# A transfer cost that counts runs of bytes, and three gate blocks early with two kept back, in the instruction order of a hybrid encoder block

## The chip, the cores and the metric

The kernel runs on one core of one Trainium2 chip. The metric is the time of the whole program in microseconds (us) on the device; lower is better. A core has five engines that each run their own list of instructions in order and wait for one another through semaphores: TensorE (PE) multiplies matrices, VectorE (DVE), ScalarE (ACT) and GpSimd (POOL) do the elementwise work, and SyncE (SP) issues the transfers (DMA).

## What is computed

One encoder block on x of 1024 positions by 1024 channels. After a normalisation and a modulation by c, one wide projection gives the inputs of two branches, a short gated convolution and a gated delta rule in both directions with 8 heads of 128; the two are merged by two sigmoid gates. Cut to what matters here:

```python
h = rmsnorm(x, norm_w) * (1.0 + scale) + shift
proj = h @ w_in
(a_bg, a_cg, a_x, a_z, q, k, v, z_b, a_raw, b_raw, gate_a_raw, gate_b_raw) = split(proj)
ya = (a_cg * dwconv_centred(a_bg * a_x, conv_a_w) * silu(a_z)) @ w_pa
q, k, v = split(silu(dwconv_centred(concat([q, k, v]), conv_qkv_w)))
q, k = l2norm(q), l2norm(k)                       # per head of 128
# per head and direction, chunks of 64 positions:
tmat = triangular_solve(eye + lower, eye)         # lower from beta, k k^T and the decays
v_new = tmat @ (v * beta) - (tmat @ (k * beta * eg)) @ state
o = (q * eg) @ state + (q k^T * decay) @ v_new
state = state * gl + (k * exp(g_last - g))^T @ v_new
yb = (rmsnorm(o_forward + o_backward) * gdn_norm_w * silu(z_b)) @ w_pb
merged = sigmoid(gate_a_raw) * ya + sigmoid(gate_b_raw) * yb
y = rmsnorm(x + gate * (merged @ w_o), final_norm_w)
```

## The kernel before

All large products are made of three matmuls, high part by high part, high by low and low by high of both operands (tiles `hhi`, `hlo`, `wh_*`, `wl_*`). A block of 128 output columns takes 48 matmuls of 128x512. Its weights come by two transfers of 256 KB (`wr_*`), ACT makes the high part (`wh_x<-wr_x`), POOL the low part (`wl_x<-wr_x,wh_x`).

The program has three stretches. In the **prologue** (to about 118 us) x is normalised, `hhi`/`hlo` are made, and the first products and decays are computed. In the **heads stage** (118 to 780 us) the 8 heads of the delta rule run. After it come the second gate's blocks, the products of the convolution branch, the two output projections and the last normalisation.

In the heads stage each head h goes through these steps, which are generators that yield PE work and hand elementwise work to the other engines:

- `prep_k`: the convolved k is transposed (`ktp`), multiplied with itself (`gram`), and DVE makes from it the matrices `N0_h`, `N1_h`. Blocks of 32 on their diagonals go by DRAM (`s1`, a first write from `N` and a second from `Vc`) into the tile `E` with another layout, where POOL inverts them in a loop of 60 instructions (`et<-E`, `E<-E,et`); the result goes back by DRAM (`s2`) into `N` and `Vb`.
- `prep_q`: products of q and k (`qk`), transposes of q (`qtp`) and of v (`vtp`, giving `vp`).
- `merge`: builds the inverse of the chunks from the small blocks: `psy`, then `psu`/`pst`, then `psz`, then `psv` on PE, each followed by copies on DVE and ACT that the next one needs.
- `chain`: the serial recurrence over 8 steps, both directions in each step (`cb`, `o`); per step PE, then DVE (`r`), PE, then ACT (`vw`, `vn`), PE, then DVE (`S`).
- `head_out`: transposes the output (`otp`), multiplies it with the gate `z` and stores it.

These steps leave PE idle when they wait for each other. What fills it are the large products: the blocks k, q, v, z of the heads in the sequence of `JOBS`, and eight blocks `ga0` to `ga7` of the first merge gate, which depend on no head. The generator `fill()` decides in `choose()` which block comes next:

```python
share = (total - START - RESERVE) * (mains - len(jobs)) / mains + START
if gates and jobs and total - len(gates) < int(share):
    return gates.pop(0)
if jobs and (len(gates) <= RESERVE or all(n in sched.done for n in jobs[0][3])):
    return jobs.pop(0)
return gates.pop(0) if gates else None
```

So `START` blocks of the gate are placed at once, `RESERVE` are kept for the end, the others are spread; a block of a head whose conditions are not met lets a gate block past while more than `RESERVE` are left, and otherwise fill() waits.

No order is written out by hand. A class `Scheduler` simulates the program while it is built: `record` takes an elementwise or DMA instruction with the cost that `Engine.cost` gives it, `step` advances the PE streams, and `run` always issues what could start first, by priority (chains and merges 0, k preparation 1, the rest 2). What it issues is the final order of the instructions of PE, DVE, ACT, POOL and SP. The numbers in `Engine.cost` therefore change no instruction, only where it stands. A transfer has two numbers: how long it holds the DMA queue, and how long after that it lands.

Of the kernel before, what the change touches and what calls it, by code (L numbers as in the profile page):

```python
# [13 lines left out]
DRAM = bass.MemoryType.DRAM  # L14
# [7 lines left out]
NEG = -1.0e30  # L22

A_BG, A_CG, A_X, A_Z, Q0, K0, V0, Z0, G_A, G_B = (8 * i for i in range(10))
START = 4
JOBS = "kqvz"
RESERVE = 3
PLAIN = (0, 4)
LAST = 6
AHEAD = 5  # L30
# [11 lines left out]
class Op:  # L42
    def __init__(self, engine, issue, cost, extra, table, port, prio, seq):
        self.engine, self.issue, self.cost, self.extra, self.table, self.port = engine, issue, cost, extra, table, port
        self.key, self.ready, self.left, self.after = (prio, seq), 0.0, 0, []
# [10 lines left out]
class Scheduler:  # L56
# [55 lines left out]
    def record(self, engine, issue, outs, ins, cost, extra, table, fill, port):  # L112
        op = Op(engine, issue, cost, extra, table, port, self.prio, self.seq)
        self.seq += 1
        op.reads = [s for ap in ins for s in self.parts(ap)]
        op.writes = [s for ap in outs for s in self.parts(ap)]
        op.fill = fill
        deps = set()
        for s in op.reads:
            op.ready = max(op.ready, self.after(engine, s.write, s.fill))  # L120
            deps.update(s.writes, s.fills)
        for s in op.writes:
            op.ready = max(op.ready, self.after(engine, s.read, s.fill))
            deps.update(s.reads, s.fills)
            if fill:
                op.ready = max(op.ready, self.after(engine, s.write))
                deps.update(s.writes)
        op.left = len(deps)
        for d in deps:
            d.after.append(op)  # L130
        for s in op.reads:
            s.reads.append(op)
        for s in op.writes:
            (s.fills if fill else s.writes).append(op)
        self.waiting += 1
        if not op.left:
            self.queue.setdefault(engine, []).append(op)
# [128 lines left out]
class Engine:  # L266


    def __init__(self, sched, name, engine):
        self._sched, self._name, self._engine = sched, name, engine  # L270

    def cost(self, op, outs, ins, kw):


        n = outs[0].free_size() / 1000.0
        if self._name == "dma":
            size = min(outs[0].nbytes(), ins[0].nbytes())
            return max(0.4, size / 360e3), 2.4 + size / 500e3, False
        if self._name == "act":
            pointers = sum(isinstance(kw.get(k), bass.AP) for k in ("bias", "scale"))  # L280
            return 0.1 + 0.83 * n + 0.07 * pointers + 0.12 * (len(outs) > 1), 0.08, False
        if self._name == "pool":
            if ALU.pow in kw.values():
                return 0.39 + 157 * n, 0.1, False
            return (0.28 + 1.93 * n if "tensor" in op else 0.06 + 0.7 * n), 0.05, op != "memset" and n > 0.03
        if op == "transpose":
            return 0.16 + 1.1 * n, 0.03, False
        both = sum(i.space != PSUM and i.free_size() == outs[0].free_size() for i in ins) > 1
        fast = op in ("tensor_copy", "tensor_scalar", "memset") and ins and ins[0].space != PSUM
        return (0.07 + 0.06 * (op == "scalar_tensor_tensor") + (0.66 if fast else 1.08 if both else 1.04) * n, 0.07,  # L290
                bool(both or fast) and n > 0.03)
# [17 lines left out]
def block(ctx: ExitStack, tc: tile.TileContext, x, c, wada, wadag, badaT, nwT, win, wab, cva, cvq,  # L309
# [753 lines left out]
    def fill():  # L1063
# [16 lines left out]
        def choose():  # L1080
# [6 lines that stand above are left out]
# [492 lines left out]
```

## Time and profile before

| | |
|---|---|
| three runs, median (lowest to highest) | 1456.3 us (1455.89 to 1461.06) |
| profiled execution | 1455.84 us |
| its span in the profile | 1453.7 us |
| TensorE clock granted in it, mean | 0.986 of full |
| busy, of the span: PE, DVE, ACT, POOL | 95%, 57%, 41%, 46% |

A line of the timeline gives start and duration in us, the engine, the line of the program, the operation, the tiles (out<-in, without their numbers), the shape, the count, and in brackets how long the engine had waited and for whom. The program's helper records nearly all elementwise and DMA instructions at line 303 and all PE work of the first two stretches at line 210, so these are told apart by their tiles. Matmuls overlap: the step from one start to the next is what one costs, not its printed duration. PEclk is the clock that TensorE was granted, 1.00 being full.

### The profile page before, as it was taken

Reading aid. Unit: us, or ns where it says so; the run is one execution under the profiler, and the core shown is the slowest. Engines: PE = TensorE matmul, PEld = TensorE weight load, DVE = VectorE, ACT = ScalarE, POOL = GpSimd, SP = SyncE. Lnnn points to the kernel's source line nnn. Section 1 sums busy time; section 2 is a strip of 40 time slices with the busy share of each in tenths; the row PEclk is TensorE's granted clock in tenths of the full one; section 3 lists DMA queues with packets and bytes.
Section 4 is the critical chain, followed back from the end, with each engine's and each line's share of the span. In section 5 each row is a group of like instructions: output and inputs, shape, how many; then the busy total and the mean of one; then the engine's idle time right before and its main releaser. Section 6 shows DMA issues by size and latency. Waiting matters only on the chain.

```text
span 1453.7 us, 22475 instructions
## 1 busy us (share of the span) xinstructions
PE 1379.9 (95%) x8510; PEld 1151.7 (79%) x8510; DVE 828.2 (57%) x1377; ACT 601.4 (41%) x1487; POOL 664.9 (46%) x847
## 2 busy tenths in 40 slices
PE   6999979899989998999799999999999999999998
PEld 5777868787878787887688878787877788888886
DVE  7677165576666766677325556565657545422235
ACT  5437538474546474644443423232232342222211
POOL 2014736663936374757315644455445413355301
PEclk9999999999999999999899999999999999999999
DMA  9233341405050423314112410303030377665402
GB/s 366 75 109 98 99 105 44 131 30 147 15 153 22 107 69 80 96 34 113 44 44 88 145 55 18 116 16 116 29 116 30 123 273 256 207 203 179 179 15 101
DMA packets 123726, 154.41 MB, mean 106 GB/s; under 512 B 74593, under 2 KB 74977, under 8 KB 123618
## 3 DMA queue, kind: packets, MB, share of 16 engines
q1 hardware_dynamic: 123330, 152.19, 33.1%
q8 instruction: 67, 1.10, 0.3%
q10 hardware_dynamic: 288, 0.79, 0.1%
q14 instruction: 41, 0.34, 0.1%
HBM read 123.45 MB, written 29.50 MB: 105 GB/s over the span
## 4 chain that ended last, share of the span: by engine, by line
PE 68%; DVE 11%; DMA 7%; ACT 5%; POOL 4%; issue 3%; SPq 2%; POOLq 0%; ACTq 0%; DVEq 0%
PE cb L210 5%; PE pp_ga L210 5%; PE pp_v L210 4%; PE pp_z L210 3%; PE ps_ax_S L1221 3%; PE o L210 3%; PE ps_cg_S L1221 3%; PE ps_bg_S L1221 3%; PE pp_q L210 3%; PE ps_az_S L1221 2%; DVE N L303 2%; PE pp_pb L1125 2%; PE pp_pb L1127 2%; PE pp_pa L1127 2%; PE pp_pa L1125 2%
## 5 line engine op out<-in xcount | busy, mean ns | idle before, releaser
L303 POOL TENSOR_TENSOR E<-E,et 128x30 f32<-128x30 f32 (+7 forms) x240 | 116.7, 486 | 17.4
L303 POOL TENSOR_TENSOR et<-E 128x30 f32<-128x30 f32 (+7 forms) x240 | 111.3, 464 | 27.9 <-DMA E<-s 11.1
L303 DVE SCALAR_TENSOR_TENSOR S<-S,exps,cb 128x128 f32<-128x128 f32 x96 | 29.8, 344 | 60.2 <-PE cb L210 59.2
L303 ACT ACTIVATE vw<-cb,cols 128x128 f32<-128x128 f32 x112 | 36.2, 364 | 57.3 <-PE cb L210 57.1
L1117 POOL TENSOR_TENSOR wl_pa<-wr_pa,wh_pa 128x512 fp32r<-128x512 f32 x16 | 27.2, 1718 | 70.2 <-ACT wh_pa L1116 55.7
L303 POOL TENSOR_TENSOR wl_ga<-wr_ga,wh_ga 128x512 fp32r<-128x512 f32 x16 | 21.2, 1328 | 79.2 <-ACT wh_ga L303 60.1
L210 PE MATMUL pp_ga<-hhi,wh_ga 128*128 128x512 f32 x128 | 51.8, 404 | 3.4 <-ACT xpad L303 3.4
L303 POOL TENSOR_TENSOR wl_q<-wr_q,wh_q 128x512 fp32r<-128x512 f32 x14 | 18.2, 1304 | 78.8 <-ACT wh_q L303 78.8
L210 PE MATMUL pp_z<-hhi,wl_z 128*128 128x512 f32 x128 | 53.0, 414 | 0.0
L210 PE MATMUL pp_z<-hhi,wh_z 128*128 128x512 f32 x128 | 53.0, 414 | 0.0
L210 PE MATMUL pp_z<-hlo,wh_z 128*128 128x512 f32 x128 | 52.6, 411 | 0.0
L210 PE MATMUL pp_ga<-hhi,wl_ga 128*128 128x512 f32 x128 | 52.2, 408 | 0.0
L210 PE MATMUL pp_ga<-hlo,wh_ga 128*128 128x512 f32 x128 | 51.7, 404 | 0.0
L303 DVE SCALAR_TENSOR_TENSOR r<-cb,negeg,vp 128x128 f32<-128x128 f32 x112 | 34.6, 345 | 29.0 <-PE cb L210 28.2
L1125 PE MATMUL pp_pb<-bhi,wh_pb 128*128 128x512 f32 x128 | 50.4, 394 | 0.0
L1127 PE MATMUL pp_pb<-bhi,wl_pb 128*128 128x512 f32 x128 | 50.2, 392 | 0.0
L1126 PE MATMUL pp_pa<-ylo,wh_pa 128*128 128x512 f32 x128 | 49.8, 389 | 0.0
L1127 PE MATMUL pp_pa<-yhi,wl_pa 128*128 128x512 f32 x128 | 49.8, 389 | 0.0
L1125 PE MATMUL pp_pa<-yhi,wh_pa 128*128 128x512 f32 x128 | 49.8, 389 | 0.0
L1126 PE MATMUL pp_pb<-blo,wh_pb 128*128 128x512 f32 x128 | 49.7, 388 | 0.0
L303 DVE SCALAR_TENSOR_TENSOR qT<-xpad,cvq_t,qT 128x1024 f32<-128x1024 f32 x32 | 46.4, 1450 | 0.4
L210 PE MATMUL pp_v<-hhi,wh_v 128*128 128x512 f32 x112 | 46.4, 414 | 0.0
(802 smaller groups left out, 4603.2 us busy)
## 6 DMA issues: line engine op xcount, KB each, us to landing
wada<-in_wada SPq DMA_DIRECT2D x16, 512.0 KB, 8.9
D<-gr_d SPq DMA_DIRECT2D x16, 512.0 KB, 7.1
xt<-in_x SPq DMA_DIRECT2D x8, 512.0 KB, 9.0
wr_k<-in_win SPq DMA_DIRECT2D x16, 256.0 KB, 2.6
wr_q<-in_win SPq DMA_DIRECT2D x16, 256.0 KB, 3.7
wr_v<-in_win SPq DMA_DIRECT2D x16, 256.0 KB, 3.4
wr_ga<-in_win SPq DMA_DIRECT2D x16, 256.0 KB, 3.3
qg<-er_d SPq DMA_DIRECT2D x8, 512.0 KB, 6.5
```

Source lines behind the costliest of these rows:

```text
L210: getattr(self.pe, what)(out, *ins, **kw)
L303: self._sched.record(self._name, lambda: real(*args, **kw), outs, ins, cost, extra, table, op == "memset", port)
L1117: G.tensor_tensor(lo[:, ch(q, 512)], raw, hi[:, ch(q, 512)].bitcast(F32), ALU.subtract)
L1125: PE.matmul(ps, wh, mhi[k][:, sl], start=i == 0, stop=False)
L1126: PE.matmul(ps, wh, mlo[k][:, sl], start=False, stop=False)
L1127: PE.matmul(ps, wl, mhi[k][:, sl], start=False, stop=i == KT - 1)
L1221: PE.matmul(ps, w[:, ch(m)], r, start=first and m == i == 0, stop=m == 3 and i == 2, skip_group_check=True)
```

## The change

```diff
-START = 4
+START = 3
 JOBS = "kqvz"
-RESERVE = 3
+RESERVE = 2
...
+    def run_of(self, ap):
+
+        n = 1
+        for step, count in reversed(ap.ap if ap.space == DRAM else ap.ap[1:]):
+            if step != n and count > 1:
+                break
+            n *= count
+        return 4 * n
+
     def cost(self, op, outs, ins, kw):
 
 
         n = outs[0].free_size() / 1000.0
         if self._name == "dma":
-            size = min(outs[0].nbytes(), ins[0].nbytes())
-            return max(0.4, size / 360e3), 2.4 + size / 500e3, False
+            size = outs[0].nbytes()
+            pieces = max(size / self.run_of(ap) for ap in (outs[0], ins[0]))
+            return max(0.4, size / 340e3, pieces / 1230), 2.4 + size / 500e3, False
```

`run_of` gives the bytes that lie next to each other in an access pattern. The queue time of a transfer in the estimate is now the largest of 0.4 us, its bytes by 340 KB per us (360 before), and its pieces by 1230 per us. The landing time is as before. Of the transfers of the heads stage, those of 128 KB in runs of 128 bytes (1024 pieces: `s1<-Vc`, two of the four `E<-s1`, the two `s2<-E`, `Vb<-s2`) go from 0.4 to 0.83 us; 256 KB go from 0.73 to 0.77, 512 KB from 1.46 to 1.54, and the small ones stay at 0.4. Early gate blocks go from four to three, kept ones from three to two. The program's arithmetic stays as it was; the order of all five engines changes from the first microseconds to the end of the heads stage, and is the same again from `gb0` on. On PE, `ga4` ran beside chain 0 and `ga5` to `ga7` at the end; now `ga3` to `ga5` stand before and beside chain 0, and `ga6` and `ga7` at the end.

Three places show it. In the rows, the first number in a name is the head (with the block for `ga`), the last a running number of the tile.

PE, chain 0 from its seventh step (index 6), before: `cb`/`o` are the chain, `pp_ga4` is the gate block that fills it.

```order
L210 MATMUL cb0_1_1801<-r0_1_6_2176,N1_0_805 128x128
L210 MATMUL pp_ga4_1_2141<-hhi3_103,wl_ga4_1714 128x512
L210 MATMUL pp_ga4_1_2141<-hhi4_444,wh_ga4_1713 128x512
L210 MATMUL pp_ga4_1_2141<-hlo4_501,wh_ga4_1713 128x512
L210 MATMUL pp_ga4_1_2141<-hhi4_444,wl_ga4_1714 128x512
L210 MATMUL pp_ga4_1_2141<-hhi5_503,wh_ga4_1713 128x512
L210 MATMUL pp_ga4_1_2141<-hlo5_504,wh_ga4_1713 128x512
L210 MATMUL pp_ga4_1_2141<-hhi5_503,wl_ga4_1714 128x512
L210 MATMUL cb0_0_1800<-vw0_0_6_2185,ktok0_799 128x128
```

The same engine in the changed kernel, from the sixth step (index 5) of chain 0 on:

```order
L210 MATMUL cb0_0_1983<-r0_0_5_2274,N0_0_804 128x128
L210 MATMUL cb0_1_1984<-r0_1_5_2277,N1_0_805 128x128
L210 MATMUL cb0_0_1983<-vw0_0_5_2284,ktok0_799 128x128
L210 MATMUL cb0_1_1984<-vw0_1_5_2288,ktok0_799 128x128
L210 MATMUL o0_1_1982<-vn0_0_5_2289,D0_0_802 128x128
L210 MATMUL o0_0_1981<-vn0_1_5_2290,D1_0_803 128x128
L210 MATMUL cb0_0_1983<-S0_0_5_2299,kT0_791 128x128
L210 MATMUL cb0_1_1984<-S0_1_5_2301,kT0_791 128x128
```

The gate block that filled these steps has ended earlier, so from the second third of step 5 to the end of step 7 nothing stands between the chain's matmuls.

ACT, merge 0 and the start of chain 0, before: `wh_ga4<-wr_ga4` is the high part of a weight block just loaded, `N<-psu0`, `T64<-pst0` and `N<-psv0` are copies of the merge.

```order
L303 ACTIVATE N0_0_804<-psu0_1645 32x8x32
L303 ACTIVATE N1_0_805<-psu0_1645 32x8x32
L303 ACTIVATE xpad0_115<-pp_v1_1_1564 128x512
L303 ACTIVATE wh_ga4_1713<-wr_ga4_0_1715 128x512
L303 ACTIVATE N1_0_805<-psv0_1770 64x8x64
L303 ACTIVATE vw0_0_0_1815<-cb0_0_1800,cols0_801 128x128
```

The same place in the changed kernel:

```order
L313 ACTIVATE wh_ga5_1719<-wr_ga5_1_1722 128x512
L313 ACTIVATE N0_0_804<-psu0_1849 32x8x32
L313 ACTIVATE T64_0_1011<-pst0_1850 32x8x32
L313 ACTIVATE N1_0_805<-psu0_1849 32x8x32
L313 ACTIVATE N1_0_805<-psv0_1957 64x8x64
L313 ACTIVATE wh_k3_1998<-wr_k3_0_2000 128x512
L313 ACTIVATE xpad1_116<-pp_ga4_1_1786 128x512
L313 ACTIVATE vw0_0_0_2006<-cb0_0_1983,cols0_801 128x128
```

No weight copy stands between the copies of the merge any more; the next one, for `k3`, stands between the merge and the chain. On SP `wr_ga4` was issued right behind the four `E1<-s1`; `wr_ga5` is issued ahead of `s1<-Vc1` and of them, `wr_k3` behind them.

PE, merge 7 to chain 7, before: from `psv7` to `cb7` six matmuls of the product `z7`.

```order
L210 MATMUL psv7_7534<-N1_7_5924,y64_7_6940 64x64
L210 MATMUL pp_z7_0_7496<-hlo4_501,wh_z7_7096 128x512
L210 MATMUL pp_z7_0_7496<-hhi4_444,wl_z7_7097 128x512
L210 MATMUL pp_z7_0_7496<-hhi5_503,wh_z7_7096 128x512
L210 MATMUL pp_z7_0_7496<-hlo5_504,wh_z7_7096 128x512
L210 MATMUL pp_z7_0_7496<-hhi5_503,wl_z7_7097 128x512
L210 MATMUL pp_z7_0_7496<-hhi6_529,wh_z7_7096 128x512
L210 MATMUL cb7_0_7553<-vp7_6857,N0_7_5923 128x128
```

The changed kernel at the end of the same stretch, whose beginning is `psv7`, two sets of `qtp7`, and `pp_z6`:

```order
L210 MATMUL otp6_1_7579<-ident_72,vp6_6369 128x128 x4
L210 MATMUL vtp7_1_7586<-ident_72,vT7_7270 128x128 x4
L210 MATMUL pp_z7_0_7592<-hhi0_100,wh_z7_7271 128x512
L210 MATMUL pp_z7_0_7592<-hlo0_104,wh_z7_7271 128x512
L210 MATMUL pp_z7_0_7592<-hhi0_100,wl_z7_7272 128x512
L210 MATMUL pp_z7_0_7592<-hhi1_101,wh_z7_7271 128x512
L210 MATMUL pp_z7_0_7592<-hlo1_105,wh_z7_7271 128x512
L210 MATMUL pp_z7_0_7592<-hhi1_101,wl_z7_7272 128x512
L210 MATMUL pp_z7_0_7592<-hhi2_102,wh_z7_7271 128x512
L210 MATMUL pp_z7_0_7592<-hlo2_106,wh_z7_7271 128x512
L210 MATMUL pp_z7_0_7592<-hhi2_102,wl_z7_7272 128x512
L210 MATMUL pp_z7_0_7592<-hhi3_103,wh_z7_7271 128x512
```

Behind these rows stands `cb7_0<-vp7`. The transposes `vtp7`, from which `vp7` is made, stood ahead of `psy7`, the merge's first product; now the last of them stands ten product matmuls ahead of it, and it is so in heads 2 to 7.

## The prediction

> **What bounds the kernel now.** First the page's busy times and the windows by stage.
>
> ```profile
> PE 1379.9 (95%) x8510; PEld 1151.7 (79%) x8510; DVE 828.2 (57%) x1377; ACT 601.4 (41%) x1487; POOL 664.9 (46%) x847
> ...
> 0.00:118.00 118.00, 97.01 (x461) 79.15 (x462) 87.33 (x149) 59.96 (x110) 18.70 (x32) 0.94 0.47 173
> 118.00:780.00 662.00, 620.41 (x5144) 532.11 (x5143) 396.66 (x835) 356.48 (x1061) 356.75 (x606) 0.98 0.30 81
> 780.00:1453.00 673.00, 662.52 (x2909) 540.40 (x2907) 344.24 (x395) 184.95 (x318) 289.43 (x210) 1.00 0.35 120
> ```
>
> PE is the bound. Its work stays, so the change can only win or lose PE's idle time and half-clock time. The last stretch keeps its order; the prologue idles 21 us, the heads stage 662.00 − 620.41 = 41.6 us, and its clock of 0.98 takes some 13 more. So the stake is 55 us, and one percent of the kernel is a quarter of it. Next, the longest of what PE waited for in heads 2 to 6 (320 to 700 us; us in total, times, longest).
>
> ```profile
> PE psz L210 <- DVE T L303: 5.7, 3, 3.0
> PE cb L210 <- DVE N L303: 3.0, 1, 3.0
> PE psu L210 <- DVE Vb L303: 2.9, 3, 1.7
> PE psv L210 <- issue: 2.9, 2, 1.5
> PE psv L210 <- ACT xpad L303: 2.8, 2, 1.5
> PE psz L210 <- ACT T L303: 1.3, 1, 1.3
> ```
>
> The idle time lies in the merges, in small pieces. In the other heads three waits are long enough to stand out; the timeline and the windows around them:
>
> ```profile
> 207.79 1.22 PE L210 MATMUL cb<-vp,N 128*128 128x128 f32 x4 [5.42 <-DVE N L303]
> 272.07 0.61 PE L210 MATMUL cb<-vw,ktok 128*128 128x128 f32 x2 [3.47 <-ACT vn L303]
> 708.26 0.31 PE L210 MATMUL psy<-T,N 32*32 32x32 f32 x2 [5.57 <-DVE T L303]
> ...
> 710.82 0.31 PE L210 MATMUL psy<-T,N 32*32 32x32 f32 x2 [1.31 <-ACT T L303]
> ```
>
> ```profile
> 207.40:211.00 3.60, 3.21 (x10) 2.76 (x11) 2.52 (x3) 2.32 (x7) 2.84 (x7) 0.53 0.22 73
> ...
> 268.00:276.00 8.00, 4.53 (x18) 3.77 (x17) 3.21 (x6) 2.77 (x7) 7.19 (x14) 0.79 1.01 345
> ...
> 707.00:717.00 10.00, 6.53 (x173) 5.37 (x174) 7.96 (x25) 2.32 (x7) 1.65 (x1) 0.55 0.15 24
> ```
>
> The clock column comes behind the instruction counts: after each long wait PE runs at about half clock, 0.53 over 3.6 us, 0.79 over 8 us, 0.55 over 10 us. The loss beside the wait is 3.6 × 0.47 = 1.7, 8 × 0.21 = 1.7, and 10 × 0.45 = 4.5 us at most (2.6 where PE had work).
>
> **Merge 0 and chain 1: weight copies in ACT's queue.** Why did `cb` wait at 207.8?
>
> ```profile
> 194.94 5.89 SPq L303 DMA_DIRECT2D E<-s  x4
> 200.87 1.06 SPq L303 DMA_DIRECT2D wr_ga<-in_win  x2
> ```
>
> ```profile
> 205.77 0.63 ACT L303 ACTIVATE wh_ga<-wr_ga 128x512 fp32r<-128x512 f32 x1 [9.49 <-POOL et L303]
> 206.43 0.59 ACT L303 ACTIVATE N<-psv 64x512 f32<-64x512 f32 x1
> ```
>
> The inferred releasers mislead (POOL, DVE). The order tells it: the merge's copy `N<-psv0` is queued behind `wh_ga4`, whose weights were issued behind the slow `E1<-s1` and landed at about 205.7. In the changed order no weight copy stands between `psu0` and `psv0`; the one ahead, `wh_ga5`, has its load issued before `E1<-s1`. `wh_k3` now stands ahead of `vw0`: it is behind `E1<-s1`, but `gram1` lies 22 us of counted PE work ahead of that use instead of 19, and DVE reaches `Vc1` without a convolution between. I take the 5.4 and the 1.7 of the clock as gone, and 0.6 us of other waits as coming back: **−6.5** (−8 to 0, if `wh_k3` is as late as `wh_ga4` was). The wait at 272 has the same cause:
>
> ```profile
> 269.99 0.63 ACT L303 ACTIVATE wh_v<-wr_v 128x512 fp32r<-128x512 f32 x1 [3.91 <-POOL E L303]
> ```
>
> `wh_v2`, also loaded behind an `E<-s`, held ACT until 270; in the changed order it stands behind `vn1`, outside the first step. That wait and its clock, −5.2, are used below.
>
> **Chain 0 unfilled.** The gate block beside chain 0 ends before step 5 does; 2⅔ steps run bare. What a bare step costs:
>
> ```profile
> 743.92 0.60 PE L210 MATMUL cb<-vw,ktok 128*128 128x128 f32 x4
> 744.37 0.61 PE L210 MATMUL o<-vn,D 128*128 128x128 f32 x4
> 745.27 0.60 PE L210 MATMUL cb<-S,kT 128*128 128x128 f32 x4
> 746.63 0.61 PE L210 MATMUL cb<-r,N 128*128 128x128 f32 x4
> ```
>
> Starts lie 1.35 us apart from `vw` to `S` and 1.36 from `S` to `r`, and 0.45 is one group (two fp32 matmuls, 0.225 each); each gap holds two groups, so 0.45 is idle, and behind `r` only one group covers the third gap, 0.9 idle if it is as long. A bare step idles 1.8 us; 2⅔ make 4.8, less what those steps idled before: **+4** (2 to 8).
>
> **psy1 comes too early for its data.** The data of a merge need the gram, the trip to `E`, the loop on POOL, the trip back. For head 1:
>
> ```profile
> 177.58 0.61 PE L210 MATMUL gram<-kT 128*128 128x128 f32 x4
> ```
>
> ```profile
> 205.48 0.24 POOL L303 TENSOR_TENSOR et<-E 128x30 f32<-128x30 f32 x1 [1.17 <-DMA E<-s]
> ...
> 242.86 0.23 POOL L303 TENSOR_TENSOR E<-E,et 128x15 f32<-128x15 f32 x1
> ```
>
> ```profile
> 254.12 0.21 PE L210 MATMUL psy<-T,N 32*32 32x32 f32 x1
> ```
>
> From gram to `E` 27 us, the loop 37.6 (two weight splits of 1.3 in or beside it), and 11 us back: 76 us; with the loop undisturbed and `Vc1` earlier 72. Counting every PE row in the changed order at its pitch (0.23 us a row of 128x512, two rows from start to start here:
>
> ```profile
> 117.67 0.39 PE L210 MATMUL pp_ga<-hhi,wl_ga 128*128 128x512 f32 x1
> ...
> 118.12 0.40 PE L210 MATMUL pp_ga<-hlo,wh_ga 128*128 128x512 f32 x1
> ```
>
> 0.225 for fp32 of 128x128), `gram1` stands at 162 us of work, `psy1` at 219; before, 144 and 209, where the clock showed 178 and 254. With the same 33.5 us lost ahead, `gram1` ends at about 196 and its data are there at 268 to 272. PE arrives at 219 + 33.5 + 7 (chain 0, merge 0) = 259.5: a wait of 8 to 12 us, so 9 (4 to 14), and 2 of clock, less the 5.2 above: **+6** (0 to +13).
>
> **Merges 2 to 6.** The six rows quoted for these heads sum to 18.6 us, about 3 each. They are hand-offs PE → DVE or ACT → PE with too little between. The changed order has product rows there in four of the five: between `psy` and `psu` 6.8, 1.6, 1.8, 11 and 3.2 us in heads 2 to 6 against some 1.5 each, between `psv` and `cb` 2.5, 4.8, 10, 7.7 and 12 against 1.5. The `psz` waits (7.0 of the 18.6) keep their thin cover of about 2 us. I take half: **−9** (−14 to 0).
>
> **Merge 7.** Before, `psy7` waits for its transfers:
>
> ```profile
> 640.93 1.05 PE L210 MATMUL gram<-kT 128*128 128x128 f32 x8
> ...
> 665.85 0.24 POOL L303 TENSOR_TENSOR et<-E 128x30 f32<-128x30 f32 x1 [1.13 <-DMA E<-s]
> ...
> 700.00 0.23 POOL L303 TENSOR_TENSOR E<-E,et 128x15 f32<-128x15 f32 x1
> 700.36 1.28 POOL L303 TENSOR_TENSOR wl_ga<-wr_ga,wh_ga 128x512 fp32r<-128x512 f32 x1
> ```
>
> 642 to 665.9, 34.4 of loop, 10.6 to `psy`: 69 us, of which PE had 55 counted and chain 6 the rest. The change puts 65.6 there, and POOL's loop has four weight splits of 1.3 in place of two, 2.6 more. Then 5.57 + 1.31 + 0.6 + 2.6 of clock, 10, fall to 3: **−7** (−10 to 0).
>
> **Smaller terms.** In the prologue `hhi`/`hlo` of the first tiles move ahead of weight splits on ACT and DVE, for which PE waited:
>
> ```profile
> 38.96 0.50 PE L210 MATMUL k<-hlo,wh_k 128*128 128x512 f32 x1 [1.20 <-DVE hlo L303]
> ```
>
> −2 (−4 to +1). Against that, `vtp` now stands 10 to 17 rows ahead of `cb` in heads 2 to 7. Behind it come four copies on ACT before `vp` is whole:
>
> ```profile
> L303 ACT ACTIVATE vp<-vtp,kss x64: 354/392/445, 139.4 to 695.6; 128x128 f32<-128x128 f32 x64
> ```
>
> 4 × 0.39 = 1.6 us under a cover of 10 to 17 × 0.23 = 2.3 to 3.9 us: nothing when ACT is free, up to 4 us a head when it is held. I take **+4** (0 to 24).
>
> Does the new cost do what it says? It lengthens the planner's path from `gram` to `psy` by 0.43 us for 128 KB in short runs, some 2.7 us a head.
>
> ```profile
> s<-E SPq DMA_DIRECT2D x16, 128.0 KB, 3.0
> ...
> s<-Vc SPq DMA_DIRECT2D x8, 128.0 KB, 5.2
> ```
>
> Queue and landing in the estimate were 3.1 for both 128 KB rows and are 3.5: better for `s<-Vc`, worse for `s<-E`. Either way it is small beside the 69 to 76 us of the path; the filler that moves comes mostly from `START` and `RESERVE`. [...]
>
> Sum: −6.5 + 4 + 6 − 9 − 7 − 2 + 4 = −10.5 from the execution's own 1455.84 (its median is 0.5 higher): **1445 us**.
>
> **Rivals.**
>
> Slower: ACT's queue. In heads 3 to 6 a weight copy (`wh_q4`, `wh_q5`, `wh_q6`, `wh_v7`) stands ahead of `vw`, or of the merge's last copy, and its load is queued right behind the four `E<-s` of the next head, the pattern that cost 5.4 us at 207.8. It decides by whether the weights land, about 27 us after the next gram (205.8 − 178.2), later than PE needs them: 19, 26, 32 and 29 us of counted work after it. Only head 3 clearly loses, and it had the pattern before. If all four lose 5.4 + 0.8 of clock, +4 becomes +25 and a little more: 1455.8 − 14.5 + 25 = 1466. Chance 0.15.
>
> No change: the bare chain and `psy1` at their upper ends, +8 and +13, the rest as taken: +0.5, **1456**. For it: the wait of `psy1` is counted, not guessed. Chance 0.28.
>
> Larger gain: `psy1`'s data are there when PE comes (+6 becomes −5) and the late `vp` costs nothing: −25.5, **1430**. Against it: 72 us are the floor in every head. Chance 0.12.
>
> **How the numbers follow.** The forecast's own case has 0.45; its terms taken half way to their ends give 1437 to 1453. The range takes in both neighbours: **1431 to 1464**. About 0.5%, 7.3 us, is what a measurement of this kernel can tell from no change. Faster by more than that, below 1449: the larger gain and most of the forecast's case, 0.53. Within: 0.30. Slower, above 1463.6: 0.17.
>
> **What would show it.** Right: no 5 us wait at chain 0's first `cb`; a wait of `psy1` of 4 to 14 us with half clock behind it; idle time of 1.8 us a step at chain 0's end; no 5 us wait at `psy7`. The prediction is wrong if `cb` in heads 3 to 6 waits for ACT, if `psy1` waits over 14 us, or if the prologue shifts by more than 4.

## The result, and the profile after

The changed kernel takes 1449.33 us (median of 6 runs, 1448.31 to 1451.39) against 1457.28 (6 runs, 1455.89 to 1461.06): a ratio of 0.9945, 95% interval 0.9929 to 0.9961, about 8 us or 0.55% faster. The profiled execution's span went from 1453.7 to 1446.7 us. The page's busy times and the windows by stage (columns as before):

```profile
PE 1385.6 (96%) x8510; PEld 1154.1 (80%) x8510; DVE 834.1 (58%) x1377; ACT 604.8 (42%) x1489; POOL 668.7 (46%) x847
...
0.00:118.00 118.00, 93.24 (x444) 77.41 (x445) 82.33 (x143) 55.27 (x101) 18.16 (x31) 0.93 0.49 173
118.00:780.00 662.00, 636.87 (x5189) 541.68 (x5189) 408.59 (x842) 366.51 (x1075) 362.88 (x609) 0.99 0.30 81
780.00:1447.00 667.00, 655.50 (x2880) 535.06 (x2878) 343.20 (x394) 183.01 (x314) 287.68 (x208) 1.00 0.35 120
```

PE's idle time in the middle window fell from 41.6 to 25.1 us, and it rose in the first 118 us from 21.0 to 24.8. These windows are fixed times, and the first `gram`, which opened the heads stage at 118 us, now comes at 126. So, for a finer reading, I took, between two marks of the program, the time from start to start of PE's rows less what each row costs undisturbed (0.2275 us for 128x512, 0.1125 for a 128x128 row, less for the small blocks). What is left is **lost time**: waiting and half clock together. A merge is counted from the first `psy` to the first `cb`, a chain from there to the next head's `psy`. Lost time is always that of the one profiled execution of a kernel, which can lie some us off the median.

| place, us lost | before | after | forecast change |
|---|---|---|---|
| prologue, to the first `gram` | 32.8 | 39.1 | −2 |
| merge 0 | 8.0 | 0.6 | −6.5 |
| chain 0, up to `psy1` | 1.8 | 3.7 | +4, and +11 for `psy1` |
| merge 1 | 1.7 | 6.9 | |
| chain 1 | 5.7 | 0.3 | −5 |
| merges 2 to 6 | 23.8 | 22.3 | −9 |
| chains 2 to 5 | 5.0 | 2.5 | |
| chain 6, up to `psy7` | 7.1 | 1.5 | −7 with merge 7 |
| merge 7 | 5.2 | 5.8 | |
| chain 7 | 0.2 | 2.6 | |
| `gram0` to `psy0`, and `gb0` to the end | 19.2 | 18.3 | 0 |
| sum | 110.5 | 103.5 | −10.5, with +4 for a late `vp` |

The three long waits of before, at their places in the changed kernel:

```profile
226.28 0.60 PE L210 MATMUL cb<-vp,N 128*128 128x128 f32 x4
```

```profile
263.43 0.24 PE L210 MATMUL psy<-T,N 32*32 32x32 f32 x2 [0.53 <-DVE T L313]
...
266.07 0.24 PE L210 MATMUL psy<-T,N 32*32 32x32 f32 x2 [1.45 <-ACT T L313]
```

```profile
694.29 0.21 PE L210 MATMUL psy<-T,N 32*32 32x32 f32 x1
...
694.78 0.24 PE L210 MATMUL psy<-T,N 32*32 32x32 f32 x2 [0.24 <-ACT T L313]
```

`cb0` starts with no wait where it had 5.42 us; `psy7` waits 0.24 where it had 5.57 and 1.31; `psy1` waits for 0.5 to 1.5 us at a time instead of the 9 that were forecast. What PE waits for in heads 2 to 6 (323 to 690 us):

```profile
PE psz L210 <- DVE T L313: 6.7, 4, 2.5
PE psv L210 <- DVE y L313: 3.8, 2, 2.1
PE pst L210 <- DVE N L313: 1.4, 2, 1.2
PE qk L210 <- DVE N L313: 0.8, 1, 0.8
```

The waits at `psu` are gone from this list and those at `cb` but for 0.2 us; those at `psz` stayed (6.7 us for 7.0), and those at `psv` fell from 5.7 to 3.8 and name another tile, `y`.

### The profile page after: what moved, and what is told of

It reads as the page before. It is cut to its first block, busy times and chain, and to the rows that moved or that the text cites. A ratio compares the mean times of both kernels' runs of the same rounds, so it can differ in the third digit from the quotient of the medians.

```text
span 1446.7 us, 22508 instructions
## 1 busy us (share of the span) xinstructions
PE 1385.6 (96%) x8510; PEld 1154.1 (80%) x8510; DVE 834.1 (58%) x1377; ACT 604.8 (42%) x1489; POOL 668.7 (46%) x847
## 4 chain that ended last, share of the span: by engine, by line
PE 77%; DVE 13%; ACT 5%; issue 2%; DMA 1%; SPq 1%; POOL 1%; POOLq 0%; ACTq 0%; DVEq 0%
PE cb L210 5%; PE pp_ga L210 5%; PE pp_k L210 5%; PE pp_q L210 5%; PE pp_v L210 4%; PE o L210 3%; PE ps_ax_S L1231 3%; PE pp_z L210 3%; PE ps_cg_S L1231 3%; PE ps_bg_S L1231 3%; PE ps_az_S L1231 2%; PE pp_pb L1135 2%; PE pp_pb L1137 2%; PE pp_pa L1136 2%; PE pp_pa L1137 2%
## 5 line engine op out<-in xcount | busy, mean ns | idle before, releaser
L313 POOL TENSOR_TENSOR et<-E 128x30 f32<-128x30 f32 (+7 forms) x240 | 115.3, 480 | 26.4 <-DMA E<-s 9.4
L313 POOL TENSOR_TENSOR E<-E,et 128x30 f32<-128x30 f32 (+7 forms) x240 | 111.4, 464 | 17.4
L313 DVE SCALAR_TENSOR_TENSOR kT<-xpad,cvq_t,kT 128x1024 f32<-128x1024 f32 x32 | 49.2, 1538 | 0.4
L210 PE MATMUL pp_k<-hhi,wh_k 128*128 128x512 f32 x112 | 46.8, 418 | 0.0
```

Of the source, the lines that this page charges most:

```text
L210: getattr(self.pe, what)(out, *ins, **kw)
L313: self._sched.record(self._name, lambda: real(*args, **kw), outs, ins, cost, extra, table, op == "memset", port)
```

## The experiments

Eleven kernels ran, each timed in five rounds against the kernel before. In the first four the change is taken apart: its two scheduling runs (prologue, heads), and its two halves (the gate blocks' counts, the transfer cost).

**The old cost in the prologue alone.**

```diff
         if self._name == "dma":
+            if self._sched.heads:
+                ...the new cost
+            ...the old cost
...
+    sched.heads = True
     sched.run([(chain(h), 0) for h in range(H)] ...
```

> The changed kernel, but its first scheduling run (the prologue) uses the old transfer cost, so that the prologue's order on all engines is that of before; heads stage with the new cost, three early, two kept. Theory: the 6.3 us that the prologue lost in the changed kernel (32.8 to 39.1 us of lost time up to the first gram) come from its new order, and the heads keep their gain: 14 us under before, about 1443 us, prologue loss 33. Rival: the prologue's loss is a matter of when transfers and clock windows happen to fall, not of the order: about 1449 us, prologue loss up to 39. A third way: the heads' order shifts too, since it starts from other times, and gives any part of their 13 us back: 1443 to 1456.

1449.6 us, ratio 0.9938 (0.9915 to 0.9961): no faster than the changed kernel. The prologue lost 34.0, as the theory has it, but the heads were scheduled from another start and got another order, with 68 us lost in place of 64. The third way; it didn't tell the first two apart.

**The new cost in the prologue alone**, the rest as before.

> The kernel before (four early, three kept, old cost in the heads), with the new transfer cost in the first scheduling run alone, so the prologue's order is that of the changed kernel. Theory: 6 us slower than before, about 1463 us, prologue loss 39. Rival (loss not due to the order): about 1457 us, prologue loss 33.

1460.45 us, 1.0022 (1.0007 to 1.0037); prologue loss 39.8, as the theory has it, and the time between the two. The loss goes with the order. The median rose by 3.0 us and the prologue's loss by 7.0; this heads order, again another, doesn't account for the difference, for it lost 79 against before's 78, though merge 0 only 2.4. The profiled execution (1463.92 us) was 3.5 slower than its median and before's 1.6 faster than its own, so the two lost times differ by more than the medians do.

**The counts alone** (three early, two kept, old cost).

> The kernel before with three gate blocks early and two kept back, the transfer cost untouched. Theory (the gain of the heads comes from where the gate blocks go): 10 to 14 us under before, 1443 to 1447 us, no 5 us wait in merge 0, none at psy7. Rival (the longer path in the estimate makes it): within 3 us of before, 1454 to 1460 us, with the long waits still there.

1460.63 us, 1.0014 (0.9997 to 1.0031): no gain, so the theory falls, and the rival, whose bounds end just below, only half holds: the long waits in merge 0 and at `psy7` did go (1.0 and 3.1 us lost), but merges 1 to 7 lost 41.4 in place of 30.7.

**The cost alone** (four early, three kept).

> The kernel before with the new transfer cost, four gate blocks early and three kept. Theory (the gain comes from the gate blocks, the prologue's loss from the cost): 3 to 8 us slower than before, 1460 to 1465 us. Rival (the new cost makes the gain): 5 to 8 us faster, 1449 to 1452 us.

1454.02 us, 0.998 (0.9963 to 0.9998): a small gain, in spite of the slow prologue (37.1 lost). Neither prediction; of the two, the rival's sign was right. So the new cost does more than the counts, against what the prediction said. The next two split it into its rate and its pieces.

**Pieces without the new rate.**

```diff
-            return max(0.4, size / 340e3, pieces / 1230), 2.4 + size / 500e3, False
+            return max(0.4, size / 360e3, pieces / 1230), 2.4 + size / 500e3, False
```

> The changed kernel with 360 KB per us kept in the estimate, so that only the term in pieces is new; three early, two kept. The prologue's order is then that of before. Theory (the prologue's loss hangs on the rate, 340 for 360, and the heads' gain on gate blocks and pieces together): prologue loss 33 to 36 us, time 1443 to 1447 us. Rival (each small change of the estimate draws another order, and the gain of the changed kernel is that of one draw): heads loss anywhere from 64 to 80 us, time 1445 to 1458.

1447.04 us, 0.9932 (0.9914 to 0.995), prologue loss 34.3: at the theory's upper end, and inside the rival's bounds as well.

**The new rate without pieces.**

```diff
-            return max(0.4, size / 340e3, pieces / 1230), 2.4 + size / 500e3, False
+            return max(0.4, size / 340e3), 2.4 + size / 500e3, False
```

> The changed kernel without the term in pieces: 340 KB per us, three early, two kept. The prologue's order is that of the changed kernel. Theory (pieces matter, since they keep the merges a little further from their grams): 4 us or more slower than the changed kernel, 1453 to 1460. Rival (pieces do nothing, the rate and the counts make the order): 1447 to 1451. If orders are drawn: 1447 to 1462.

1475.76 us, 1.0125 (1.0104 to 1.0146), more than any expectation: 26 us slower than the changed kernel, which has one term more. What stands out is POOL in head 6, whose `E` is ready at 607 and whose result is sent off at 670:

```profile
606.92 0.12 POOL L313 MEMSET E<- 64x16 f32 x1 [11.89 <-DMA E<-s]
...
636.84 1.39 POOL L313 TENSOR_TENSOR wl_z<-wr_z,wh_z 128x512 fp32r<-128x512 f32 x1 [7.21 <-ACT wh_z L313]
639.59 1.28 POOL L313 TENSOR_TENSOR wl_z<-wr_z,wh_z 128x512 fp32r<-128x512 f32 x1
...
651.20 1.29 POOL L313 TENSOR_TENSOR wl_q<-wr_q,wh_q 128x512 fp32r<-128x512 f32 x1 [1.48 <-ACT wh_q L313]
...
664.77 1.29 POOL L313 TENSOR_TENSOR wl_v<-wr_v,wh_v 128x512 fp32r<-128x512 f32 x1
```

```profile
669.97 1.27 SPq L313 DMA_DIRECT2D s<-E  x2
```

The loop takes 62 us, against 39 in the changed kernel's head 6: weight splits of the products stand between its instructions, and POOL, working in order, waits in the loop for weights that ACT has not converted. But this loop cost PE no wait: `psy6` starts at 681.9 with its data there, as `psy2` of the kernel before does behind a loop of 60 us. Chains 4 to 6 lost 26 us here and 2.5 in the changed kernel, and PE's longest wait in the heads is at `psy7`, whose loop takes 37 us:

```profile
741.33 0.31 PE L210 MATMUL psy<-T,N 32*32 32x32 f32 x2 [8.95 <-DVE T L313]
...
744.50 0.31 PE L210 MATMUL psy<-T,N 32*32 32x32 f32 x2 [1.55 <-ACT T L313]
```

From the last `gram` of head 7 to its `psy` this order has 49 us of PE work, the changed one 66. In chain 4, `psy5` waits 2.7 us behind a loop of 56 us, and in chain 5 a `cb` waits 3.8 us for `vn`, behind a weight copy `wh_v` on ACT whose load SP had issued behind the four `E<-s`. Of what is lost, then, little is shown to hang on the stretched loops.

**One exchange in SP's queue.** The kernel before, all engines in its order, but the loads of `wr_ga4` issued ahead of the four `E1<-s1`.

```diff
+BEHIND = (('E1_', 'wr_ga4_1'),)
...
+        self.late = []
...
+    def emit(self, name, run):
+        for late, first in BEHIND:
+            if name.startswith(late):
+                self.late.append(run)
+                return
+        run()
+        for late, first in BEHIND:
+            if name.startswith(first):
+                for r in self.late:
+                    r()
+                self.late = []
...
```

> The kernel before with one thing exchanged in SP's queue and nothing else on any engine: the two loads of the weights of ga4 are issued ahead of the four reads of E by head 1, not behind them. Theory: the wait of 5.4 us at the first cb of chain 0 was that load, so the wait falls under 1 us and the lost time from psy0 to cb0 from 8.0 to 1 to 2 us. What becomes of it: either it stays, 6 to 7 us under before (about 1451), or psy1, which came when its data were just there, waits for them instead and half or more is given back (1453 to 1457). Rival (the wait is for DVE or POOL, as the releaser in the row says): the wait stays at 5 us and the time within 1 us of before.

1452.76 us, 0.997 (0.9955 to 0.9985). ACT's timeline at the place, then PE's first `cb` and its `psy1`:

```profile
201.50 0.63 ACT L317 ACTIVATE wh_ga<-wr_ga 128x512 fp32r<-128x512 f32 x1 [4.22 <-DMA wr_ga<-in_win]
202.16 0.59 ACT L317 ACTIVATE N<-psv 64x512 f32<-64x512 f32 x1
```

```profile
203.75 0.71 PE L224 MATMUL cb<-vp,N 128*128 128x128 f32 x4 [0.38 <-DVE N L317]
```

```profile
250.71 0.24 PE L224 MATMUL psy<-T,N 32*32 32x32 f32 x2 [1.61 <-ACT T L317]
```

The weights land 4 us earlier, ACT's copy follows, the wait falls to 0.38 and the lost time of merge 0 from 8.0 to 3.0 (1 to 2 were expected). This shows the cause of the long wait: not POOL or DVE, which the rows named, but a load queued behind others. And it shows the price: merge 1, which had come when its data were just there, now loses 5.1 in place of 1.7. Of the 5.0 in merge 0 and 1.3 in chain 0, 3.4 went back there; the medians differ by 4.3. That lies between the two outcomes that the theory left open.

**The changed kernel's heads behind the old prologue.** The order of the second scheduling run was written down from the changed kernel as a table and replayed, so that the heads' instructions stand in the same order on every engine.

```diff
+            if plan:
+                n = plan.pop(0)
+                if n < 100:
+                    pick = next(s for s in live if s[3] == n)
+                    ...
+                else:
+                    op = next(op for ops in self.queue.values() for op in ops if op.key[1] - base == n - 100)
+                    ...
+                continue
```

> The prologue scheduled with the old transfer cost, so in the order of before, and the heads stage in exactly the order of the changed kernel, instruction by instruction on all engines. Theory (the prologue's loss is in its order): prologue loss 33 to 36 us, the heads as in the changed kernel (25 us lost from the first gram to gb0 without the waits that hang on transfers), 3 to 6 us under the changed kernel, 1443 to 1446. Rival (the heads lose what the prologue wins, since transfers of weights come later against the chains): 1448 to 1451.

1444.63 us, 0.9914 (0.9893 to 0.9934), beside 0.9945 (0.9929 to 0.9961) of the changed kernel. Prologue 31.8 lost (33 to 36 were expected), and the rest 66.5 against 64.4, place by place within 0.9 us of the changed kernel (merge 1: 6.9 and 6.9). The theory holds: the prologue's order costs some 5 us, and the heads don't mind it. (The 25 us of the expectation for the heads was a slip; the changed kernel loses 47.6 from the first gram to `gb0`.) In this pair of executions the lost time of the heads goes with the order. It is one pair: executions of one kernel differ more (1438.25 to 1448.67 us here), and this pair doesn't show where.

**Two by two, dose, and where the price is put.** The fourth cell of the table of counts and pieces at the old rate:

> Only the term in pieces is new: four gate blocks early, three kept back, 360 KB per us, prologue in the order of before. With the runs so far it closes a table of two by two at the old rate: neither (before, 1457), counts alone (1460.6), both (1447.0), and this one, pieces alone. Theory 1 (the pieces make the gain and the counts add a little): 1449 to 1452. Theory 2 (it takes both): 1455 to 1459. Theory 3 (orders are drawn): outside both.

1449.59 us, 0.9943 (0.9922 to 0.9965): theory 1. Twice the price (`pieces / 615`):

> As the kernel with pieces alone at the old rate and three early, two kept (1447.0), but with twice the price: pieces / 615, 1.67 us for 1024 pieces. Theory (distance between gram and psy is what helps): the lost time in the merges and at psy7 falls further, 1440 to 1446. Rival (0.83 us was about right, and more pushes psy so late that chains start with nothing beside them): 1448 to 1456. If orders are drawn: anything from 1445 to 1465.

1451.03 us, 0.9957 (0.9936 to 0.9977): inside the rival's bounds, and those for drawn orders. Twice the price gives no more. And the price as landing time:

```diff
-            return max(0.4, size / 360e3, pieces / 1230), 2.4 + size / 500e3, False
+            return max(0.4, size / 360e3), 2.4 + size / 500e3 + max(0.0, pieces / 1230 - max(0.4, size / 360e3)), False
```

> As the kernel with pieces at the old rate and three early, two kept (1447.0), but the price of the pieces is put on the landing of a transfer and not on the time that it holds the queue: the path from gram to psy is as long in the estimate, the queue as free as before. Theory (the longer path is what helps): 1445 to 1449. Rival (the queue's time is what helps, since it moves weight loads against the reads of E): 1455 to 1462.

1444.11 us, 0.9899 (0.9871 to 0.9927), the lowest ratio of all and a little under the theory's bounds; the price need not stand in the queue's time.

The combinations of pieces, counts and rate, with the lost time in five places. It is that of one execution each; that of the fifth row took 1451.5 us, 4.5 more than its median, and that of the third 4.8 more.

| kernel | pieces | counts | rate | us | ratio | prologue | merge 0 | merges 1–7 | chains 0–5, 7 | chain 6 |
|---|---|---|---|---|---|---|---|---|---|---|
| before | no | 4/3 | 360 | 1457.3 | 1 | 32.8 | 8.0 | 30.7 | 12.7 | 7.1 |
| counts alone | no | 3/2 | 360 | 1460.6 | 1.0014 | 36.6 | 1.0 | 41.4 | 17.4 | 3.1 |
| rate, counts | no | 3/2 | 340 | 1475.8 | 1.0125 | 40.6 | 0.6 | 40.2 | 22.7 | 12.1 |
| pieces alone | yes | 4/3 | 360 | 1449.6 | 0.9943 | 31.0 | 3.8 | 27.7 | 11.3 | 12.4 |
| pieces, counts | yes | 3/2 | 360 | 1447.0 | 0.9932 | 34.3 | 0.5 | 31.0 | 14.2 | 8.8 |
| pieces, rate | yes | 4/3 | 340 | 1454.0 | 0.998 | 37.1 | 1.7 | 31.1 | 8.6 | 11.5 |
| changed | yes | 3/2 | 340 | 1449.3 | 0.9945 | 39.1 | 0.6 | 35.0 | 9.1 | 1.5 |

The three pairs that differ in pieces alone say the same: −0.57%, −0.8% and −1.8% of before's time with them. The counts give nothing that can be told without pieces (+0.14%) and with them at the old rate (0.9932 and 0.9943, intervals that overlap), and some 0.35% at the new rate. The rate costs: 5 us in the prologue, and the heads change with it.

## Why the prediction came out as it did

The time lies inside the range and near the forecast, faster by 8 us for 10.5; but several terms were off and cancelled, so that it came so near is in good part luck. Of the prediction's own signs, the waits of 5 us at chain 0's first `cb` and at `psy7` went, as they should; the wait of `psy1` and the idle steps of chain 0 did not come in the size named; and the prologue shifted by more than 4 us, which it had named as a sign of being wrong.

**Prologue, −2: wrong in sign, +6.3.** The step that failed took the moves of `hhi` and `hlo` ahead of weight splits for a gain and didn't ask what moved back. In the changed order of DVE, `hlo1` and `hlo2` stand ahead of reductions of the `wada` tiles, from which the scale of a later hidden tile comes. PE's waits at the start, before and in the changed kernel:

```profile
PE xtp L210 <- DVE dg L303: 9.1, 1, 9.1
...
PE k L210 <- ACT hhi L303: 3.1, 2, 2.5
PE k L210 <- DVE hlo L303: 2.1, 3, 1.2
PE tab L210 <- DVE sp L303: 1.9, 1, 1.9
```

```profile
PE xtp L210 <- DVE dg L313: 9.5, 1, 9.5
PE k L210 <- ACT hhi L313: 3.6, 2, 2.5
PE k L210 <- DVE hlo L313: 3.0, 3, 1.1
PE tab L210 <- DVE sp L313: 2.9, 1, 2.9
```

They grew by 2.8 us together, and PE got less clock behind them. Two windows of 9 us of the kernel before, and the same two places in the changed one:

```profile
83.00:92.00 9.00, 9.00 (x41) 7.42 (x41) 7.23 (x9) 1.56 (x4) 1.46 (x1) 0.81 0.19 58
110.00:119.00 9.00, 6.72 (x26) 5.56 (x27) 8.14 (x12) 8.97 (x20) 3.16 (x3) 0.81 0.03 11
```

```profile
84.00:93.00 9.00, 6.52 (x25) 5.93 (x26) 4.81 (x8) 0.59 (x2) 2.19 (x2) 0.62 0.01 2
115.00:124.00 9.00, 6.91 (x18) 5.47 (x19) 7.94 (x12) 8.95 (x21) 3.15 (x3) 0.62 0.04 15
```

The clock fell from 0.81 to 0.62, so half of each window's loss is new, 1.7 us. That the order makes it is shown by the replay, and by two groups of kernels: with the old prologue's order on the four other engines nine profiles lost 31.0 to 37.0 us (mean 33.8), with the new one four lost 37.1 to 40.6 (39.2). The single profiles nearly touch, so one alone would not tell. Which of the moved instructions does it was not tried.

**Merge 0 and chain 1, −6.5 and −5: right.** They measured −7.4 and −5.4, and the exchange in SP's queue shows the mechanism for the first; for the second no run was made. It has a condition that the text didn't see: merge 0 lost 0.3 to 3.8 us in every other order. The long wait was one of before's order, and each change of the estimate that was tried ended it.

**Chain 0, +4: right way, mis-sized, by a misreading.** It lost 1.9 more. I took the time between four quoted rows as idle; product rows that I had left out lay between them. The steps that really are bare, in the changed kernel:

```profile
248.48 0.60 PE L210 MATMUL cb<-vw,ktok 128*128 128x128 f32 x4
248.92 0.61 PE L210 MATMUL o<-vn,D 128*128 128x128 f32 x4
249.37 0.68 PE L210 MATMUL cb<-S,kT 128*128 128x128 f32 x4
...
250.33 0.65 PE L210 MATMUL cb<-r,N 128*128 128x128 f32 x4
251.76 0.74 PE L210 MATMUL cb<-vw,ktok 128*128 128x128 f32 x4 [0.78 <-ACT vn L313]
```

From `vw` to `vw` 3.28 us for 2.25 of work: 1.0 lost a step, not 1.8. The only real gap is behind `cb<-r`, where ACT makes `vw`.

**psy1, +11 ahead of chain 1's −5: the step failed.** Its wait was 0.5 us and a few of up to 1.5, not 9. The data's way was taken from before's head 1, 72 to 76 us. In the changed kernel:

```profile
201.60 1.95 PE L210 MATMUL gram<-kT 128*128 128x128 f32 x16
```

```profile
223.27 0.24 POOL L313 TENSOR_TENSOR et<-E 128x30 f32<-128x30 f32 x1 [2.46 <-DMA E<-s]
...
255.30 0.23 POOL L313 TENSOR_TENSOR E<-E,et 128x15 f32<-128x15 f32 x1
```

20 us to `E` in place of 27, the loop 32 in place of 37.6, 8 back in place of 11: 60 in all. The way isn't a floor; it goes through the queues of DVE, SP and POOL, and what stands in them differs with the order. In before's head 1 the four reads of `E` took 5.9 us on SP and a weight split in the loop waited 3.5 us for ACT; here the reads took 2.6, and none of the four splits in the loop waited. A part came back in merge 1, which lost 5.2 more, in hand-offs and 3.4 us of half clock:

```profile
266.50:270.00 3.50, 3.49 (x64) 2.74 (x64) 1.50 (x7) 2.00 (x10) 0.12 (x1) 0.52 0.78 126
```

**Merges 2 to 6, −9: mis-sized, −1.5.** Product rows between `psy` and `psu` and between `psv` and `cb` removed the waits at those two, as worked out, and `psz` waits on, as expected. PE's waits in these merges fell from 20.1 to 13.4 us, not far from the term; but 3.6 us came back as half clock, in windows from 416.7 (merge 3) and 641.9 us (merge 6), while before's, from 429.3, had fallen into chain 3, and 1.6 in steps without a shown wait. The step counted waits alone and no clock.

**psy7, −7: right in mechanism**, −5.0 (chain 6 −5.6, merge 7 +0.6). **Late vp, +4: no cost seen**; `cb` in heads 2 to 6 waits for ACT 0.2 us in all, so the slower rival's mechanism did not come either. Chain 7 lost 2.4 more, which nothing in the prediction had.

**That the filler moves mostly by the counts: wrong.** The prediction called the new cost small beside a path of 69 to 76 us, and gave pieces no price of its own. The runs show the reverse: pieces alone make the whole gain, counts alone none. Whether the number fits the chip, which the prediction weighed (3.5 in the estimate, 3.0 and 5.2 measured), was beside the point: in this program the number acts through the order alone. Why this term gives better orders stays open. All orders of the scheduler without pieces lost 78 to 95 us outside the prologue, all with them 64 to 73; the price works as landing time as well, and twice as much gives no more. A longer way in the estimate should set the merges further from their grams, but the orders bear that out in part only: the PE work from a head's last `gram` to its first `psy`, mean of the 8 heads, rises with pieces in the three pairs (72.7 to 73.4 us from the kernel before, 74.0 to 75.6 with the new counts, 69.3 to 75.6 with the new rate too), but the fastest kernel has 71.6, less than the kernel before. That pieces help as such, and did not only draw better orders here, is not shown.

## What to carry to other kernels

A number in a scheduler's estimate is judged by the order that comes out, not by its size beside the real duration: 0.43 us a transfer was worth 8 to 26 us here, and a rate changed by 6% cost 5 us in a part that nobody had looked at. Change one number at a time and time each, since parts of a change can have opposite signs, as the pieces and the rate had; and once a good order is found, it can be written down and replayed, which keeps it while another part is changed. Where an engine works in order, look in its queue ahead of a late instruction for one that waits for a transfer: the row's releaser may name another engine. And where an estimate of the gain counts waits alone, ask where the half-clock windows will fall.

## What was not expected of the hardware

An order replayed behind another prologue lost the same time at the same places, within 0.9 us in each of 18 stretches, though all of it came 6 to 7 us earlier and one of the four half-clock windows in the heads fell into another merge (from 416.7 us, in merge 3, to 486.7 us, in merge 4). And the first transfers vary more than that from one execution to another: PE's first wait, for `dg`, was 9.1 to 10.9 us among kernels with the same order up to there.
